# Reversed tables by wide copies, batches every 5.5 ticks, and the final weight on ScalarE, in a Hymba-style layer

## The chip, the cores and the metric

The kernel runs on one core of a Trainium2 chip (trn2). The core has TensorE for matrix products (PE in the profile, its weight loads PEld), VectorE (DVE), ScalarE (ACT), GpSimd (POOL) and SyncE (SP), which issues the DMAs; each has its own instruction stream and they meet at semaphores. The metric is the device time of one execution in microseconds (us). The kernel before ran three times: 1730.94, 1727.21 and 1730.14 us, median 1730.14.

## The reference

One decoder layer in float32, one batch of 1024 tokens, model width 1024, FFN width 2816. The code below is cut to what is computed.

```python
mod = silu(cond) @ w_mod + b_mod                       # 9 vectors: shift, scale, gate of 3 sub-layers
h = modulate(rms_norm(x, ffn1_norm), sh1, sc1)
x = x + 0.5 * g1 * ((silu(h @ w_gate) * (h @ w_up)) @ w_down)

h = modulate(rms_norm(x, mix_norm), sh2, sc2)
b_gate, c_gate, v, u = split(h @ w_in)                 # four parts of width 512
y_conv = b_gate * conv3_causal(c_gate * v)
y_ssm = s5_mixer(u)                                    # state_t = A state_{t-1} + B u_t, then GELU and a gate (GLU)
y_mix = concat(rms_norm(y_conv, out_norm_conv), rms_norm(y_ssm, out_norm_ssm))
x = x + g2 * (y_mix @ w_out)

h = modulate(rms_norm(x, ffn2_norm), sh3, sc3)
x = x + 0.5 * g3 * ((silu(h @ ffn2_w_gate) * (h @ ffn2_w_up)) @ ffn2_w_down)
return rms_norm(x, final_norm)
```

The S5 mixer has 32 groups of 16 channels with 64 complex states each. Its matrices depend only on weights (lambda, log_dt, B and C), so they can be made before `u` is known.

## The kernel before, in words

Activations lie transposed: eight tiles `xt` of x, in pairs, each of 128 features by 512 tokens for either half `h` of the tokens. The products run as three passes with operands split into a high and a low part (`mm3`: high by high, high by low, low by high), so a product of a 512-wide tile is 3 matmuls, and a sum over four tiles of features is 12.

The gate and up products of the first FFN go by a Strassen-Winograd scheme of seven products in place of eight (`seven`). A group of the FFN's width (fa0 to fa10 in the names, fb0 to fb10 for the second FFN) has seven products for the gate and seven for the up part, named by their blocks: fa5gB, fa5gD, fa5gA, fa5gE, fa5gC and so on. Each goes into a PSUM bank, and VectorE adds the banks together (`fa5gu<-fa5gt,fa5gB`); while a sum is still to be read, its bank is not free for the product that comes two or more later. The weights come by DMA as `raw`; GpSimd makes the sums of blocks that the scheme needs (the lines L165, L166, L174 and L176 of the profile); ScalarE casts each to a high part (`CAST w<-raw`), and VectorE subtracts this from `raw` for the low part (`TENSOR_TENSOR w<-raw,w`).

Nothing is reordered by a scheduler. The engine handles V, A, SP and T are wrapped by `InOrder`, which makes each instruction follow the one recorded before it on its engine, so an instruction stands behind all that the program gave to its engine earlier; every wrapped instruction bears the line of that helper in the profile, L108. What the order is made by is `Clock` (L60 to L100): one tick is one `mm3`. At each tick the clock runs what is due (`clock.after(ticks, fn)`), and at every `period` ticks it takes one step of the generators in `clock.side`. A group is 56 ticks, and each tick is 3 matmuls.

In the first FFN the side generator is `side1`: after the inputs' combinations it runs `ssm_base`, which makes the tables of the state-space model, and then `ssm_batch` for eight batches of four groups of channels each. `ssm_base` computes powers `pw` of the states' factors on VectorE and writes four tables `tab0` to `tab3` with ScalarE, two of them in the order of the powers and two reversed. `ssm_batch` builds its operands `cl` and `bl` (from the tables and the parameters `prm` and `bb`), asks TensorE for the products `kp` and for transposes `tp`, and rotates matrices (`rot`, `rott`); `dg` and `kc` put the diagonal in, and the results go to DRAM. The period is 4.5 ticks for all of this, and 2 from the last group's first half on.

In the second FFN's last down product (`fb10d`) the tail is made by `after2`: for each tile of x that is done, ScalarE squares it (`Sumsq.add`), and the squares are summed by GpSimd or VectorE and then by TensorE with a vector of ones (`st`). `roots` makes the reciprocal root in nine small VectorE instructions, `wide` spreads it over 128 columns (`rb`), and `spread` transposes it on TensorE into PSUM (`bc`). Then `put` multiplies each tile of x by the final weight (a column of `cols`) and by `bc`, and every second tile is followed by the DMA of both to the output. The first half of the tokens (n_0) is one piece of 512; the second is two pieces of 256, which the profile calls n_0 (128x256) and n_256.

Of the kernel before, what the change touches and what calls it, by code (L numbers as in the profile page):

```python
# [13 lines left out]
F32 = mybir.dt.float32  # L14
F32R = mybir.dt.float32r
I32 = mybir.dt.int32
AF = mybir.ActivationFunctionType
ALU = mybir.AluOpType
# [3 lines left out]
P = 128  # L22
D = 1024
S = 1024
HALF = 512
# [72 lines left out]
class InOrder:  # L98
# [4 lines left out]
    def __init__(self, tc, engine):  # L103
        self.tc, self.engine, self.last = tc, engine, None

    def __getattr__(self, name):
        def call(*args, **kw):
            r = getattr(self.engine, name)(*args, **kw)  # L108
            if self.last is not None and InOrder.strict:
                info = mybir.DependencyInfo(mybir.DependencyClass.NoSync, mybir.DependencyReason.DATA)  # L110
                self.tc.add_manual_dep(r.ins, self.last.ins.name, info, reason="order of issue")
            self.last = r
            return r

        return call
# [117 lines left out]
def hymba_layer(ctx: ExitStack, tc, x_d, wm1_d, wmod_d, gu1_d, gs1_d, ds1_d, wl1_d, win_d, wout_d, glu_d, gu2_d, gs2_d, wd2_d, ds2_d, wl2_d, cols_d, cond_d, lam_d, bc_d, out_d):  # L233
# [160 lines left out]
    def roots(st, q, width, nm):  # L394
# [13 lines left out]
        return y  # L408

    def wide(y, nm):  # L410

        q = y.shape[1]
        rb = t2k(nm + "rb")[:, : q * P].rearrange("p (a b) -> p a b", a=q)
        V.tensor_scalar(out=rb, in0=y.unsqueeze(2).to_broadcast([P, q, P]), scalar1=0.375, scalar2=None, op0=ALU.mult)
        return rb
# [528 lines left out]
    def ssm_base(sb, sb1):  # L944
# [114 lines left out]

        tabs = [sb.tile([P, 9, G], F32, tag=f"tab{i}", name=f"tab{i}") for i in range(4)]  # L1060
        for n, (t, (top, ts_, bot, bs_)) in enumerate(zip(tabs, ((0, 1, 1, -1), (1, -1, 0, -1), (0, 1, 1, 1), (1, -1, 0, 1)))):
            for part, i, sg in ((lo, top, ts_), (hi, bot, bs_)):
                if n < 2:
                    A.activation(t[part], pw[part, i], AF.Copy, scale=float(sg))
                else:

                    for q in range(8):
                        A.activation(t[part, q, :], pw[part, i, 7 - q, :], AF.Copy, scale=float(sg))
                yield
        zero = sb1.tile([CH, 112], F32, name="zero")  # L1070
# [135 lines left out]
    def side1():  # L1206
        yield from combos1()
        sb = side_open.enter_context(tc.tile_pool(name="sb", bufs=1, side="right"))
        with tc.tile_pool(name="sb1", bufs=1, side="right") as sb1:
            yield from ssm_base(sb, sb1)  # L1210
        bps.append(side_open.enter_context(tc.tile_pool(name="bp", bufs=1, side="right")))
        mod_home.pool = side_open.enter_context(tc.tile_pool(name="wmp", bufs=1, side="right"))
        for _ in range(2):
            mod_fetch(mod_home)
        for b in range(NB):
            yield from ssm_batch(b)
# [42 lines left out]
    movs["B"] = es1.enter_context(tc.tile_pool(name="movB1", bufs=12))  # L1259
    LAST_PERIOD = 2  # L1260
    sums_open, first_open = ExitStack(), ExitStack()
# [374 lines left out]
    down7("fbd1", lefts[1], 2, fetch_last)  # L1636
    n4 = {}
    WHOLE = [slice(0, HALF)]
    PIECES = (WHOLE, [slice(0, HALF // 2), slice(HALF // 2, HALF)])

    def after2(d, h, tok):
# [3 lines left out]
        ss = n4[h, tok.start]  # L1645
        ss.add(x[d][h][:, tok], apart=d == KT - 1, beside=d < 6)

        def put(k, bc):
            xs = x[k][h][:, tok]
            V.scalar_tensor_tensor(out=xs, in0=xs, scalar=cols[:, C_NF + k : C_NF + k + 1], in1=bc[:, :n], op0=ALU.mult, op1=ALU.mult)  # L1650
            if k % 2:
                SP.dma_start(out_d[h, :, k - 1 : k + 1, tok], xt[k // 2][h][:, :, tok])

        def use(bc):
            for k in range(KT):
                clock.after(2 * k, lambda k=k: put(k, bc))

# [96 lines left out]
```

## Time and profile before

| what | value |
| --- | --- |
| median of three runs | 1730.14 us (1727.21 to 1730.94) |
| the profiled execution | 1728.82 us |
| its span, first to last instruction | 1727.0 us |
| mean granted TensorE clock | 0.989 of full speed |
| busy: PE, PEld, DVE, ACT, POOL | 1661.6, 1368.2, 1263.0, 604.6, 373.8 us |
| DMA | 281.47 MB, mean 163 GB/s |

The profile has a page (busy times, slices, groups of instructions) and answers on the trace. In a row of the timeline stand the start, the time, the engine, the line, the operation, and output and inputs with their shapes; a count x12 says that so many equal instructions in a row are one row; in brackets stands the idle time of the engine before it and what ended it. Instructions on an engine overlap a little: the next one starts before the previous one's time is over. In the rows of waits stand the total, the count and the longest. In the rows of windows each engine's busy time is followed by its count; PEclk is the granted clock, 1.00 is full speed.

### The profile page before, as it was taken

Reading aid. Unit: us, or ns where it says so; the run is one execution under the profiler, and the core shown is the slowest. Engines: PE = TensorE matmul, PEld = TensorE weight load, DVE = VectorE, ACT = ScalarE, POOL = GpSimd, SP = SyncE. Lnnn points to the kernel's source line nnn. Section 1 sums busy time; section 2 is a strip of 40 time slices with the busy share of each in tenths; the row PEclk is TensorE's granted clock in tenths of the full one; section 3 lists DMA queues with packets and bytes.
Section 4 is the critical chain, followed back from the end, with each engine's and each line's share of the span. In section 5 each row is a group of like instructions: output and inputs, shape, how many; then the busy total and the mean of one; then the engine's idle time right before and its main releaser. Section 6 shows DMA issues by size and latency. Waiting matters only on the chain.

```text
span 1727.0 us, 20694 instructions
## 1 busy us (share of the span) xinstructions
PE 1661.6 (96%) x7484; PEld 1368.2 (79%) x7484; DVE 1263.0 (73%) x1994; ACT 604.6 (35%) x1032; POOL 373.8 (22%) x290
## 2 busy tenths in 40 slices
PE   4999999989999999999999899999999999999997
PEld 3787788878878878887877778888888888888886
DVE  7939789997589997644666877967776767676646
ACT  4225433333354332332113324533434443322221
POOL 0012232332322221100000021123223223332211
PEclk9999999999999999999999999999999999999998
DMA  8122364454564656225654452314444344659312
GB/s 326 77 98 96 131 217 156 153 186 136 213 210 151 228 183 253 67 69 151 208 164 135 150 186 90 141 49 171 177 190 170 147 156 161 260 227 375 112 49 98
DMA packets 101624, 281.47 MB, mean 163 GB/s; under 512 B 19345, under 2 KB 34961, under 8 KB 90386
## 3 DMA queue, kind: packets, MB, share of 16 engines
q1 hardware_dynamic: 101522, 280.15, 46.2%
q8 instruction: 59, 0.97, 0.2%
q14 instruction: 43, 0.35, 0.1%
HBM read 195.69 MB, written 76.02 MB: 157 GB/s over the span
## 4 chain that ended last, share of the span: by engine, by line
PE 48%; DVE 5%; DMA 3%; issue 1%; ACT 0%; SPq 0%; POOL 0%; DVEq 0%; ACTq 0%
PE wo L108 2%; PE fb10d L108 2%; PE u L108 2%; PE fbd_1B L108 2%; PE fbd_0B L108 2%; PE b L108 2%; PE v L108 1%; DMA swz<-si 1%; PE fb0u L108 1%; PE fbd_0A L108 1%; PE fb0g L108 1%; PE fbd_1C L108 1%; PE fbd_0C L108 1%; PE fbd_1A L108 1%; PE fb0d L108 1%; DMA wm<-in_wmod 1%
## 5 line engine op out<-in xcount | busy, mean ns | idle before, releaser
L108 ACT CAST w<-raw 128x512 fp32r<-128x512 f32 (+1 forms) x374 | 240.5, 677 | 474.8 <-issue 78.2
L108 DVE TENSOR_TENSOR w<-raw,w 128x512 fp32r<-128x512 f32 (+1 forms) x374 | 307.8, 843 | 123.0 <-ACT w L108 122.4
L174 POOL TENSOR_TENSOR raw<-sums,raw 128x512 f32<-128x512 f32 x54 | 81.3, 1505 | 415.4 <-DVE w L108 403.1
L165 POOL TENSOR_TENSOR sums<-raw 128x512 f32<-128x512 f32 x54 | 77.5, 1435 | 332.2 <-DMA raw<-in_gs 162.9
L176 POOL TENSOR_TENSOR raw<-raw 128x512 f32<-128x512 f32 x54 | 83.5, 1548 | 92.6 <-DVE w L108 92.6
L108 DVE CUSTOM_DVE_ANT_0 wm<-wm,cact 128x1024 f32<-128x1024 f32 x56 | 78.1, 1408 | 10.3 <-DMA wm<-in_wmod 10.2
L166 POOL TENSOR_TENSOR raw<-raw 128x512 f32<-128x512 f32 x54 | 84.5, 1564 | 4.2
L367 POOL TENSOR_TENSOR n3aq<-n3aq,n3aq 128x512 f32<-128x512 f32 x5 | 7.6, 1529 | 278.4 <-ACT n3aq L108 278.2
L108 PE MATMUL p<-h,w 128*128 128x512 f32 x192 | 49.2, 420 | 7.7 <-DVE h L108 5.4
L108 DVE TENSOR_TENSOR w<-sums,w 128x512 fp32r<-128x512 f32 x54 | 55.0, 1030 | 1.6 <-ACT w L108 1.0
L108 PEld LDWEIGHTS p<-h,w 128*128 128x128 f32 x192 | 38.9, 204 | 17.9 <-DVE h L108 6.4
L108 PE MATMUL wo<-oa,w 128*128 128x512 f32 x192 | 46.1, 393 | 1.2 <-DVE w L108 0.7
L108 PE MATMUL v<-h,w 128*128 128x512 f32 x192 | 46.8, 395 | 0.0
L108 PE MATMUL c<-h,w 128*128 128x512 f32 x192 | 46.6, 394 | 0.0
L108 PE MATMUL u<-h,w 128*128 128x512 f32 x192 | 45.9, 399 | 0.2 <-DVE h L108 0.2
L108 PE MATMUL b<-h,w 128*128 128x512 f32 x192 | 45.6, 393 | 0.0
L108 PE MATMUL wo<-ob,w 128*128 128x512 f32 x192 | 45.3, 391 | 0.0
L108 ACT CAST w<-sums 128x512 fp32r<-128x512 f32 x54 | 32.8, 621 | 34.5 <-PE fa9gE L108 2.2
L108 PEld LDWEIGHTS wo<-oa,w 128*128 128x128 f32 x192 | 35.7, 188 | 9.7 <-DVE w L108 1.1
L108 PEld LDWEIGHTS u<-h,w 128*128 128x128 f32 x192 | 36.3, 191 | 8.5 <-DVE h L108 0.6
L108 PEld LDWEIGHTS wo<-ob,w 128*128 128x128 f32 x192 | 35.8, 188 | 7.3
L108 PEld LDWEIGHTS b<-h,w 128*128 128x128 f32 x192 | 35.5, 188 | 7.2
(1579 smaller groups left out, 4004.4 us busy)
## 6 DMA issues: line engine op xcount, KB each, us to landing
raw<-in_gs SPq DMA_DIRECT2D x38, 1024.0 KB, 5.4
wm<-in_wmod SPq DMA_DIRECT2D x56, 512.0 KB, 4.9
raw<-in_ds SPq DMA_DIRECT2D x16, 1024.0 KB, 6.3
mw<-in_wm SPq DMA_DIRECT2D x8, 1024.0 KB, 12.4
x<-in_x SPq DMA_DIRECT2D x16, 512.0 KB, 9.0
raw<-in_win SPq DMA_DIRECT2D x8, 1024.0 KB, 5.4
raw<-in_gu SPq DMA_DIRECT2D x6, 1024.0 KB, 10.2
raw<-in_wl SPq DMA_DIRECT2D x5, 1024.0 KB, 6.5
```

What stands on the lines that cost most here:

```text
L108: r = getattr(self.engine, name)(*args, **kw)
L165: self.G.tensor_tensor(out=f, in0=r[2], in1=r[1], op=ALU.subtract)
L166: self.G.tensor_tensor(out=r[1], in0=r[1], in1=r[0], op=ALU.subtract)
L174: self.G.tensor_tensor(out=r, in0=s["t3"], in1=r, op=ALU.add)
L176: self.G.tensor_tensor(out=r, in0=self.chunk(j, 3), in1=r, op=ALU.subtract)
L367: nc.gpsimd.tensor_tensor(out=a, in0=a, in1=sq[:, :n], op=ALU.add)
```

## The change

There are three edits. First, the two reversed tables: before, 32 small ScalarE instructions of 64x32 each read one power at a time; now eight copies of 128x2x32 fill a tile `pd` with the powers in reversed order, and four instructions of 64x256 write the tables from it. The generator yields twice among the copies and after each table, 6 times instead of 8. Second, from the end of `ssm_base` the side period is 5.5 ticks instead of 4.5. Third, in the tail ScalarE multiplies each finished tile by the final weight right behind its square, so `put` is one multiplication by `bc` for a pair of tiles (128x1024, or 128x2x256) and the pair's DMA; the squares of the seventh tile are added by GpSimd; and the writing of the second half's first piece is split, with its last two pairs made to follow the last piece's `rb`.

```diff
     class InOrder
+    def follow(self, r, before):
+        info = mybir.DependencyInfo(mybir.DependencyClass.NoSync, mybir.DependencyReason.DATA)
+        self.tc.add_manual_dep(r.ins, before.ins.name, info, reason="order of issue")
...
     def wide(y, nm):
-        V.tensor_scalar(out=rb, in0=y.unsqueeze(2).to_broadcast([P, q, P]), scalar1=0.375, scalar2=None, op0=ALU.mult)
+        r = V.tensor_scalar(out=rb, in0=y.unsqueeze(2).to_broadcast([P, q, P]), scalar1=0.375, scalar2=None, op0=ALU.mult)
+        widened.append(r)
         return rb
...
         tabs = [sb.tile([P, 9, G], F32, tag=f"tab{i}", name=f"tab{i}") for i in range(4)]
+        down_ = sb1.tile([P, 2, 8, G], F32, tag="pd", name="pd")
+        for q in range(8):
+            A.copy(down_[:, :, q, :], pw[:, :, 7 - q, :])
+            if q % 4 == 3:
+                yield
         for n, (t, (top, ts_, bot, bs_)) in enumerate(zip(tabs, ((0, 1, 1, -1), (1, -1, 0, -1), (0, 1, 1, 1), (1, -1, 0, 1)))):
             for part, i, sg in ((lo, top, ts_), (hi, bot, bs_)):
                 if n < 2:
                     A.activation(t[part], pw[part, i], AF.Copy, scale=float(sg))
                 else:
-
-                    for q in range(8):
-                        A.activation(t[part, q, :], pw[part, i, 7 - q, :], AF.Copy, scale=float(sg))
-                yield
+                    A.activation(t[part, 0:8, :], down_[part, i], AF.Copy, scale=float(sg))
+            yield
...
             yield from ssm_base(sb, sb1)
+        clock.period = BATCH_PERIOD
...
-    LAST_PERIOD = 2
+    LAST_PERIOD, BATCH_PERIOD = 2, 5.5
...
-        ss.add(x[d][h][:, tok], apart=d == KT - 1, beside=d < 6)
-
-        def put(k, bc):
-            xs = x[k][h][:, tok]
-            V.scalar_tensor_tensor(out=xs, in0=xs, scalar=cols[:, C_NF + k : C_NF + k + 1], in1=bc[:, :n], op0=ALU.mult, op1=ALU.mult)
-            if k % 2:
-                SP.dma_start(out_d[h, :, k - 1 : k + 1, tok], xt[k // 2][h][:, :, tok])
+        xs = x[d][h][:, tok]
+        ss.add(xs, apart=d == KT - 1, beside=d < 7)
+        A.activation(xs, xs, AF.Copy, scale=cols[:, C_NF + d : C_NF + d + 1])
+
+        def put(j, bc):
+            pair = xt[j][h][:, :, tok]
+            r = V.tensor_tensor(out=pair, in0=pair, in1=bc[:, :n].unsqueeze(1).to_broadcast([P, 2, n]), op=ALU.mult)
+            if h and tok.start == 0 and j > 1:
+                V.follow(r, widened[-1])
+            if h and tok.start and j == 0:
+                V.follow(r, put_last[-1])
+            put_last.append(r)
+            SP.dma_start(out_d[h, :, 2 * j : 2 * j + 2, tok], pair)

         def use(bc):
-            for k in range(KT):
-                clock.after(2 * k, lambda k=k: put(k, bc))
+            back = 7 if h and tok.start == 0 and n < HALF else 2
+            for j in range(KT // 2):
+                clock.after((1 if back > 2 else 4) * j + back, lambda j=j: put(j, bc))
```

The order of the program shows three places. On ScalarE, where the tables are made during group fa3, before (the names are those of the tables `tab`, the powers `pw` and the split weights `w`; the number behind a name is a buffer's):

```order
L108 COPY fa3gt_1321<-fa3gA 128x512
L108 ACTIVATE tab_1523<-pw 64x288
L108 ACTIVATE tab_1524<-pw 64x288
L108 ACTIVATE tab_1523<-pw 64x288
L108 CAST w_1344<-raw_1039 128x512
L108 CAST w_1344<-raw_1165 128x512
L108 ACTIVATE tab_1524<-pw 64x288
L108 ACTIVATE tab_1525<-pw 64x32 x16
L108 ACTIVATE tab_1526<-pw 64x32 x16
L108 CAST w_1400<-raw_1165 128x512 x2
```

and now:

```order
L112 COPY fa3gt_1321<-fa3gA 128x512
L112 ACTIVATE tab_1523<-pw 64x288
L112 ACTIVATE tab_1524<-pw 64x288
L112 COPY pd<-pw 128x2x32 x2
L112 CAST w_1344<-raw_1039 128x512
L112 CAST w_1344<-raw_1165 128x512
L112 COPY pd<-pw 128x2x32 x6
L112 ACTIVATE tab_1523<-pw 64x288
L112 ACTIVATE tab_1524<-pw 64x288
L112 ACTIVATE tab_1525<-pd 64x256 x2
L112 ACTIVATE tab_1526<-pd 64x256 x2
L112 CAST w_1400<-raw_1165 128x512 x2
```

Between the two pairs of casts stood 33 instructions, and there are 12 now.

On VectorE, at the first batch's second block in group fa5 (`dg` to `clt` are the batch's; the two `fa5gu` additions and `fa5gt` read the banks of that group's products), before:

```order
L108 TENSOR_SCALAR gate<-gate 128x8
L108 TENSOR_TENSOR fa5gu_2094<-fa5gu_2079,fa5gD 128x512
L108 TENSOR_TENSOR w_2098<-raw_1838,w_2098 128x512
L108 TENSOR_TENSOR fa5gt_2030<-fa5gu_2094,fa5gC 128x512
L108 TENSOR_TENSOR w_2098<-raw_1838,w_2098 128x512
L108 TENSOR_TENSOR dg_2162<-ident,lam 16x64
L108 TENSOR_TENSOR bb_2194<-prm_2191,qq 128x128
L108 TENSOR_TENSOR kc_2160<-kc_2160,dg_2162 16x4x16
L108 TENSOR_TENSOR bb_2195<-prm_2191,qq 128x128
L108 TENSOR_TENSOR bb_2193<-bb_2194,bb_2195 128x64 x2
L108 TENSOR_TENSOR cl_2200<-tab_1523,prm_2191 128x576
L108 TENSOR_TENSOR clt_2201<-tab_1524,prm_2191 128x576
```

and now:

```order
L112 TENSOR_SCALAR gate<-gate 128x8
L112 TENSOR_TENSOR dg_2130<-ident,lam 16x64
L112 TENSOR_TENSOR bb_2172<-prm_2169,qq 128x128
L112 TENSOR_TENSOR kc_2128<-kc_2128,dg_2130 16x4x16
L112 TENSOR_TENSOR bb_2173<-prm_2169,qq 128x128
L112 TENSOR_TENSOR bb_2171<-bb_2172,bb_2173 128x64 x2
L112 TENSOR_TENSOR cl_2178<-tab_1523,prm_2169 128x576
L112 TENSOR_TENSOR clt_2179<-tab_1524,prm_2169 128x576
L112 TENSOR_TENSOR fa5gu_2088<-fa5gu_2060,fa5gD 128x512
L112 TENSOR_TENSOR w_2092<-raw_1835,w_2092 128x512
L112 TENSOR_TENSOR fa5gt_2015<-fa5gu_2088,fa5gC 128x512
L112 TENSOR_TENSOR w_2092<-raw_1835,w_2092 128x512
```

The batch's block has moved from behind `fa5gt` to ahead of it. Over the whole first FFN the batches' products `kp` stand 22 to 36 ticks apart before, three of them in group fa7, and 27 to 44 apart now, two at most in a group.

On VectorE at the program's end (the last two pieces; `n_1_0` and `n_1_256` are the program's names for what the profile calls n_0 and n_256), before:

```order
L108 SCALAR_TENSOR_TENSOR x_1_3800<-x_1_3800,cols,n_1_0bc 128x256
L108 SCALAR_TENSOR_TENSOR n_1_256ny<-n_1_256na,n_1_256ni 128x2
L108 SCALAR_TENSOR_TENSOR x_1_3800<-x_1_3800,cols,n_1_0bc 128x256
L108 TENSOR_TENSOR n_1_256na<-n_1_256ny 128x2
L108 TENSOR_TENSOR n_1_256na<-n_1_256na,n_1_256nv 128x2
L108 SCALAR_TENSOR_TENSOR n_1_256na<-n_1_256na 128x2
L108 SCALAR_TENSOR_TENSOR n_1_256ny<-n_1_256na,n_1_256ny 128x2
L108 TENSOR_SCALAR n_1_256rb<-n_1_256ny 128x256
L108 SCALAR_TENSOR_TENSOR x_1_3797<-x_1_3797,cols,n_1_256bc 128x256 x2
```

and now:

```order
L112 SCALAR_TENSOR_TENSOR n_1_256ny<-n_1_256na,n_1_256ny 128x2
L112 TENSOR_SCALAR n_1_256rb<-n_1_256ny 128x256
L112 TENSOR_TENSOR x_1_3780<-x_1_3780,n_1_0bc 128x2x256
L112 TENSOR_TENSOR x_1_3781<-x_1_3781,n_1_0bc 128x2x256
L112 TENSOR_TENSOR x_1_3778<-x_1_3778,n_1_256bc 128x2x256
```

The multiplications of the second half's first piece, which stood between the steps of the last piece's root, now stand half ahead of them and half behind `rb`.

More of the change, by code (lines that the diff above doesn't have):

```diff
@@ L109, in call @@
             if self.last is not None and InOrder.strict:
-                info = mybir.DependencyInfo(mybir.DependencyClass.NoSync, mybir.DependencyReason.DATA)
-                self.tc.add_manual_dep(r.ins, self.last.ins.name, info, reason="order of issue")
+                self.follow(r, self.last)
             self.last = r
@@ L408, in roots @@
         return y
+    widened = []
     def wide(y, nm):
@@ L1636, in hymba_layer @@
     down7("fbd1", lefts[1], 2, fetch_last)
-    n4 = {}
+    n4, put_last = {}, []
     WHOLE = [slice(0, HALF)]
```

## The prediction

> **What bounds the kernel now.** I read the page's busy times first, then the waits of TensorE, then a timeline at each long wait. TensorE:
>
> ```profile
> span 1727.0 us, 20694 instructions
> PE 1661.6 (96%) x7484; PEld 1368.2 (79%) x7484; DVE 1263.0 (73%) x1994; ACT 604.6 (35%) x1032; POOL 373.8 (22%) x290
> ...
> PE kp L108 <- DVE bl L108: 4.5, 2, 4.2
> ...
> PE fa3gC L108 <- DVE fa3gt L108: 3.4, 1, 3.4
> ...
> PE fad_0A L108 <- DVE w L108: 2.7, 2, 2.0
> ```
>
> TensorE is busy for 1661.6 of 1727.0 us, so whatever an edit saves must come out of the 65.4 us in which it idles, out of time in which it runs at a lower clock, or out of what follows its last matmul. The change adds and removes no multiplication on TensorE. Two of its places stand in these rows (wait in total, count, longest): `kp`, a batch's products, and `fa3gC`, both waiting for VectorE. The third is the tail. I take the three in turn.
>
> **Tables (first edit).** In the timeline around 181 us ScalarE makes the four tables while TensorE wants a bank:
>
> ```profile
> 181.32 4.60 ACT L108 ACTIVATE tab<-pw 64x288 f32<-64x288 f32 x33
> ...
> 181.71 2.88 PE L108 MATMUL fa3gE<-h,w 128*128 128x512 f32 x12
> ...
> 185.94 1.14 ACT L108 CAST w<-raw 128x512 fp32r<-128x512 f32 x2
> 186.59 0.69 DVE L108 TENSOR_TENSOR w<-raw,w 128x512 fp32r<-128x512 f32 x1 [2.85 <-ACT w L108]
> ...
> 187.20 0.68 DVE L108 TENSOR_TENSOR fa3gt<-fa3gu,fa3gC 128x512 f32<-128x512 f32 x1
> ...
> 188.03 4.41 PE L108 MATMUL fa3gC<-h1S,w 128*128 128x512 f32 x12 [3.44 <-DVE fa3gt L108]
> ...
> 190.58 1.76 DVE L108 TENSOR_TENSOR w<-raw,w 128x512 fp32r<-128x512 f32 x1
> ...
> 192.23 3.11 PE L108 MATMUL fa3uA<-h,w 128*128 128x512 f32 x12
> ...
> 195.18 1.07 PE L108 MATMUL fa3uC<-h1S,w 128*128 128x512 f32 x4
> ```
>
> The weight casts wait on ScalarE behind 33 small instructions (4.60 us). VectorE, in its order, stands at the `w` that needs the cast (2.85 us idle) with `fa3gt` behind it, and TensorE's second `fa3gC` needs the bank that `fa3gt` reads. Then the clock falls. In the windows (TensorE's busy time first, granted clock as PEclk near the end of a row):
>
> ```profile
> 190.00:192.00 2.00, 2.00 (x6) 1.54 (x6) 2.00 (x2) 0.59 (x2) 1.79 (x2) 0.50 0.15 31
> ...
> 388.00:390.00 2.00, 1.73 (x8) 1.01 (x8) 1.97 (x4) 0.00 (x0) 0.00 (x0) 0.50 0.72 295
> ...
> 392.00:394.00 2.00, 2.00 (x7) 1.52 (x6) 1.46 (x3) 1.69 (x4) 0.00 (x0) 0.50 0.71 162
> ...
> 620.00:622.00 2.00, 1.47 (x6) 1.24 (x7) 2.00 (x3) 0.00 (x0) 1.91 (x2) 1.00 0.00 0
> ```
>
> After 3.44 us of idling it is 0.50 at 190 to 192; after the 2.0 us of `fad_0A`, which ended at 620.5, it stayed 1.00. Twelve matmuls at full clock take 2.72 us (fa5gE to fa5gC below, 264.77 to 267.50). From 188.03 to 195.18 two sets took 7.15 us in place of 5.44: 1.71 lost to the clock, with the idling 5.15 us in all.
>
> What the new order costs, by the two groups that ran in that stretch (busy time, mean of one):
>
> ```profile
> L108 ACT ACTIVATE tab<-pw 64x32 f32<-64x32 f32 x32 | 4.2, 213 | 0.0
> ...
> L108 ACT ACTIVATE tab<-pw 64x288 f32<-64x288 f32 x4 | 1.7, 438 | 5.3 <-DVE pw L108 5.2
> ```
>
> Back to back, 32 elements take 4.2/32 = 0.131 us and 288 take 1.7/4 = 0.425. On the line between them 64 elements (one `pd` copy) take 0.17 and 256 take 0.39. Between the two pairs of casts now stand six copies, two 288s and four 256s: 6×0.17 + 2×0.425 + 4×0.39 = 3.4 us instead of 4.6; ahead of the first pair two copies replace one 288 (0.34 for 0.425). The casts start 1.2 + 0.1 = 1.3 us earlier, VectorE was waiting for nothing else, and the idling falls from 3.44 to about 2.1. That is next to the 2.0 that kept the clock, so I take 2.1 as the whole loss: **gain 3.0**. Bounds: 1.3 if the clock falls all the same, 5.15 if nothing of the wait is left. The two yields that fall away move the batches' start by a tick or two only; the second edit sets the period from there.
>
> The Trainium skill, "TensorE: Matmul & The Clock Gate", Part 1, says that the clock is halved after an idle window of about 3.4 us and that the window runs freely, which the 3.44 here fits, and the 3.53 in the tail; by a free-running window a 2.1 us gap is mostly, not surely, safe. No sum uses it.
>
> **Batches (second edit).** A batch of the SSM's matrices is spread over steps between the matmuls, with about 10 us of VectorE. Windows of one group of 168 matmuls each (the third figure after the comma is VectorE's, with its count):
>
> ```profile
> 211.50:249.60 38.10, 38.10 (x170) 31.55 (x169) 32.51 (x50) 12.10 (x21) 12.18 (x7) 1.00 0.60 208
> 249.60:290.80 41.20, 41.20 (x193) 33.52 (x192) 39.96 (x61) 14.16 (x25) 13.05 (x9) 1.00 0.50 173
> 290.80:332.00 41.20, 41.20 (x188) 33.81 (x187) 36.68 (x60) 13.55 (x24) 12.64 (x8) 1.00 0.47 154
> 332.00:373.70 41.70, 41.38 (x199) 33.29 (x198) 39.85 (x64) 15.29 (x27) 12.47 (x8) 1.00 0.52 158
> 373.70:424.60 50.90, 46.71 (x205) 37.57 (x204) 40.53 (x69) 16.56 (x29) 13.43 (x9) 0.93 0.44 142
> 424.60:459.99 35.39, 35.39 (x157) 29.28 (x156) 20.29 (x30) 10.32 (x18) 11.32 (x8) 1.00 0.68 260
> ```
>
> The last has no batch: 20.29 in 35.39, or 21.8 in the 38.1 of a group. The five with batches hold 189.5, less 5×21.8 leaves 80.5 for eight batches, 10 each (some of that is the gates' rows). Before, group fa7 holds three batches' products: 21.8 + 30 = 52 of VectorE in a stretch of some 42, so VectorE falls behind, and the next batch's product pays:
>
> ```profile
> 386.97 1.16 DVE L108 TENSOR_TENSOR bl<-bl,blt 128x512 f32<-128x512 f32 x1
> ...
> 388.27 1.86 PE L108 MATMUL kp<-cl,bl 128*16 128x128 f32 x8 [4.19 <-DVE bl L108]
> ```
>
> Idle 4.19 us, then half clock from 388.3 to 394 (rows above): half of 5.7 is 2.9. With the other wait of `kp` (4.5 − 4.2 = 0.3) the loss is 7.4; the sets that were not quite at half speed take about 0.3 off it, so 7.1. At 5.5 ticks a step no group holds more than two products: 21.8 + 20 = 42 in about 41. That is level, not behind. I take all 7.1 as gained; bounds 0 (VectorE falls behind elsewhere) and 7.4. The batches end some 15 us later, in the stretch of the last window above where VectorE is 57% busy, and the next thing that needs their results comes only after this stage; I cost that at nothing, and were that cover gone it would show as a wait of the mixer.
>
> What the new steps meet: the order shows the first batch's block (`dg`, `bb`, `kc`, `bb`, `bb` twice, `cl`, `clt`) now ahead of the additions that free the bank of the second `fa5gC`; before it stood behind them.
>
> ```profile
> 262.36 1.29 POOL L174 TENSOR_TENSOR raw<-sums,raw 128x512 f32<-128x512 f32 x1 [10.28 <-DVE w L108]
> ...
> 264.77 2.88 PE L108 MATMUL fa5gE<-h,w 128*128 128x512 f32 x12
> 264.98 0.68 DVE L108 TENSOR_TENSOR fa5gt<-fa5gu,fa5gC 128x512 f32<-128x512 f32 x1
> ...
> 267.50 2.88 PE L108 MATMUL fa5gC<-h1S,w 128*128 128x512 f32 x12
> ...
> 268.13 2.52 DVE L108 TENSOR_TENSOR bb<-bb,bb 128x64 f32<-128x64 f32 x2
> ...
> 338.47 0.21 DVE L108 TENSOR_TENSOR dg<-ident,lam 16x64 f32<-16x64 f32 x1
> ...
> 341.12 1.29 DVE L108 TENSOR_TENSOR w<-raw,w 128x512 fp32r<-128x512 f32 x2
> ```
>
> The same block undisturbed took 341.12 − 338.47 = 2.65 us. `fa5gt` ended at 265.66; with the block ahead it ends at 268.3, and `fa5gC`, ready at 267.50, waits 0.9 with the release. But GpSimd works around this time (its addition of 262.36 ends at 263.65, and others follow), and two-input work of VectorE is at times longer: the `bb` pair here took 2.52 us, as much as the whole block elsewhere, and the `w` of 190.58 took 1.76 where that of 186.59 took 0.69, 1.1 more. With one such stretch between the block and `fa5gt` the wait is 0.9 + 1.1 = 2.0 to 2.05, which I take (2.05), since the block itself would mostly run in the gap behind 263.65. Bounds: 0.9, and 5 if the whole block is stretched as the `bb` pair was (2.2 more) with the clock falling. Net of this edit: 7.1 − 2.05 = **5.05**.
>
> The Trainium skill, "GPSIMD Engine Reference", says that GpSimd shares its SBUF interfaces with VectorE, and that two-SBUF-input instructions of VectorE contend; the rows agree (1.76 against 0.69), though they do not say which of its instructions did it, and no number above needs it.
>
> **The tail (third edit).** VectorE's end, after TensorE's last product:
>
> ```profile
> 1715.92 0.15 DVE L108 TENSOR_SCALAR n_256nv<-n_256st 128x2 f32<-128x2 f32 x1
> ...
> 1718.41 0.16 DVE L108 TENSOR_TENSOR n_256na<-n_256na,n_256nv 128x2 f32<-128x2 f32 x1
> ...
> 1719.00 0.29 DVE L108 TENSOR_SCALAR n_256rb<-n_256ny 128x256 f32<-128x256 f32 x1
> ...
> 1719.35 1.22 PE L108 MATMUL n_256bc<-ident,n_256rb 128*128 128x128 f32 x4 [3.53 <-DVE n_256rb L108]
> 1720.61 3.22 DVE L108 SCALAR_TENSOR_TENSOR x<-x,cols,n_256bc 128x256 f32<-128x256 f32 x8 [1.32 <-PE n_256bc L108]
> ```
>
> Between 1715.92 and 1719.00 nine small instructions of the root alternate with multiplications of the previous piece; the change sends two of the four paired ones behind `n_256rb`. Uninterleaved, nine follow each other at 0.2 us, as the last three before `n_256rb` do (1718.41 to 1719.00): 1716.2 + 1.8 = 1718.0 (1716.2 since the two paired writes ahead end some 0.3 later). `n_256bc` arrives 1719.65, and four multiplications of 512 elements, each about 0.6 apart (`fa5gt`, which also reads PSUM, started 264.98 and took 0.68, of which some 0.08 overlaps the next), end at 1722.1 rather than 1720.61 + 3.22 = 1723.83. The two pairs moved behind lie in the wait for `n_256bc`. The span ends 3.17 us after the last multiplication, for the transfers; the same transfers now start closer together, so not all of the 1.7 reaches the end: **gain 1.5**, bounds 0 (transfers decide) and 2.2. ScalarE's 24 added multiplications (a pair of its 512-wide casts took 1.14, so some 0.6 each) lie beside 2.72 us of matmuls per tile; the addition moved to GpSimd also ends before its piece's sums.
>
> **The sum.** 3.0 + 5.05 + 1.5 = 9.55 us off the span, 1727.0 to 1717.4. The profiled execution took 1728.82, 1.8 around its span and 1.3 under the median of 1730.14; so about 1719.3 for such an execution and 1730.14 − 9.55 = **1720.5** for a median.
>
> **The rivals.** Prices are against 1730.14 or the forecast.
>
> (1) *The clock still falls at the tables* (the gate's rule above says when): gain 1.3 there, not 3.0; 1722.3. For it: 2.1 is above 2.0, the only gap seen to be harmless. Chance 0.15.
>
> (2) *The wait at fa5gC is 5 us, or one like `kp`'s returns once more* as VectorE stays level but not ahead: 3 to 7 us more; 1723.5 to 1727.5. For it: two batches need 42 in 41. Against: a group without batches follows. Chance 0.2.
>
> (3) *Slower.* Blocks of a batch stand ahead of bank-freeing additions in every group, not in fa5 alone. Each such place that idles TensorE over 3.4 us costs 5.15, as at the tables. Without the wait at fa5gC the forecast would be 1718.45; three such places make 1733.9, which is slower by the bound below, four 1739.1. For it: the steps fall at other places of a group each time. Against: `fa5gt` ended 1.8 us before `fa5gC` was ready, so a block of 2.65 alone costs only 0.9. Chance 0.06.
>
> (4) *The tail is bound by transfers and the batches' gain is as forecast*: 1722.0. Chance 0.1, inside the range.
>
> **How the numbers follow.** The forecast itself (1717 to 1722) has 0.49. The range runs from all terms at their good end (5.15 + 7.4 − 0.9 + 2.2 = 13.9, 1716.3; some 1.3 more for the spread of the runs, 1727.21 to 1730.94, so 1715) to most of rival 2: 1726. What a measurement of this kernel can tell from no change is 0.2%, 3.5 us: faster means below 1726.7. Faster 0.82 (forecast 0.49, rivals 1 and 4 0.25, the lower part of rival 2, 0.08), same 0.12 (its upper part), slower 0.06.
>
> **What would show it.** Right: `fa3gC`'s wait near 2.1 and clock 1.00 at 188 to 194; no wait of `kp` over 1 us; a new wait of `fa5gC` near 2; `n_256rb` near one us earlier relative to `n_256nv`. Wrong: a row of 0.50 after the tables, a `kp` or bank wait over 3.4 us in fa5 to fa9, or a span that ends as long after `n_256bc` as before.

## The result and the profile after

The changed kernel took 1721.68 us, the median of five runs (1719.28 to 1722.76), against 1730.14 of the kernel before (1727.21 to 1730.94, five runs). The ratio is 0.9951, with a 95% interval of 0.9937 to 0.9966: faster by 8.5 us. The forecast was 1720.5, within 1715 to 1726. One later execution of the changed kernel ran at a clock of 0.656 throughout and took 2395.23 us; it stands outside every comparison. The profiled execution took 1719.28, its span 1717.5.

The page's first lines of the profile after:

```profile
span 1717.5 us, 20689 instructions
...
PE 1657.8 (97%) x7484; PEld 1365.9 (80%) x7484; DVE 1262.0 (73%) x1979; ACT 616.0 (36%) x1036; POOL 375.3 (22%) x293
```

VectorE has as much to do as before (1262.0 us for 1263.0); what fell is TensorE's time, idle (59.7 for 65.4) and busy at a low clock. TensorE's waits in the profile after (total, count, longest):

```profile
PE n_0bc L112 <- DVE n_0rb L112: 2.4, 1, 2.4
...
PE fa3gC L112 <- DVE fa3gt L112: 2.3, 1, 2.3
PE n_256bc L112 <- DVE n_256rb L112: 2.2, 1, 2.2
...
PE fa10uC L112 <- DVE fa10ut L112: 2.0, 1, 2.0
...
PE fa5gC L112 <- DVE fa5gt L112: 1.5, 1, 1.5
```

`kp` is gone from the list, `fa3gC` is 2.3 for 3.4, and `fa5gC` is new: the three things that the prediction named. `fa10uC` with 2.0 was not foreseen. For the comparison by place I cut each profiled execution at five instructions that stand in all of them, by their starts in the timeline: the first fa3gA, the first fa5gA, the first fa9uA, the first `wo` (the output projection of the mixer) and TensorE's last product fb10d. In us:

| stretch | before | after | first edit alone | the same, steps put back | block behind fa5gt | period 5.0 |
| --- | --- | --- | --- | --- | --- | --- |
| fa3gA to fa5gA (tables) | 81.46 | 78.70 | 78.68 | 78.71 | 80.22 | 78.73 |
| fa5gA to fa9uA (batches) | 191.38 | 185.77 | 193.06 | 190.73 | 184.00 | 196.82 |
| fa9uA to wo | 511.57 | 513.17 | 511.98 | 514.24 | 510.66 | 520.65 |
| wo to the last product | 758.64 | 756.57 | 756.59 | 757.06 | 758.39 | 759.42 |
| last product to the end | 15.84 | 15.30 | 16.49 | 15.75 | 14.5 | 14.46 |

Between before and after the batches give 5.6, the tables 2.8 and the tail 0.5; and of the two stretches between, which no edit touches, one loses 1.6 and the other gains 2.1. The rows behind the first three, in the timeline of the profile after:

```profile
182.96 1.69 ACT L112 ACTIVATE tab<-pd 64x256 f32<-64x256 f32 x4
184.67 1.14 ACT L112 CAST w<-raw 128x512 fp32r<-128x512 f32 x2
185.32 0.69 DVE L112 TENSOR_TENSOR w<-raw,w 128x512 fp32r<-128x512 f32 x1 [1.73 <-ACT w L112]
...
186.76 2.97 PE L112 MATMUL fa3gC<-h1S,w 128*128 128x512 f32 x12 [2.28 <-DVE fa3gt L112]
...
260.90 0.20 DVE L112 TENSOR_TENSOR dg<-ident,lam 16x64 f32<-16x64 f32 x1
...
262.87 0.75 DVE L112 TENSOR_TENSOR clt<-tab,prm 128x576 f32<-128x576 f32 x1
263.54 0.68 DVE L112 TENSOR_TENSOR fa5gu<-fa5gu,fa5gD 128x512 f32<-128x512 f32 x1
...
264.14 1.35 DVE L112 TENSOR_TENSOR w<-raw,w 128x512 fp32r<-128x512 f32 x1
...
265.42 0.68 DVE L112 TENSOR_TENSOR fa5gt<-fa5gu,fa5gC 128x512 f32<-128x512 f32 x1
...
266.24 3.00 PE L112 MATMUL fa5gC<-h1S,w 128*128 128x512 f32 x12 [1.49 <-DVE fa5gt L112]
...
344.41 1.05 PE L112 MATMUL kp<-cl,bl 128*16 128x128 f32 x8
```

The casts start at 184.67 for 185.94. The `fa3gC` behind them takes 2.97 us for its twelve matmuls where it took 4.41 before: the clock stayed up. The batch's block (260.90 to 263.54, 2.64 us) stands ahead of fa5gt, one `w` is stretched to 1.35, and TensorE idles 1.49. The products `kp` come with no idle time before them.

The two stretches that no edit touches differ by where the clock fell. In the profile after it fell behind the 1.96 us of `fa10uC`, in the third stretch (timeline):

```profile
488.98 4.47 PE L112 MATMUL fa10uC<-h1S,w 128*128 128x512 f32 x12 [1.96 <-DVE fa10ut L112]
```

Before, this wait was 0.88 and the twelve matmuls took 3.00. The order of work is the same there; what came late is a transfer. ScalarE's cast of a weight, which had waited for its DMA, started 0.52 us behind the start of `fa10uE`, where it had started 0.57 ahead of it before (484.66 and 484.14 after, 492.06 and 492.63 before), and `fa10ut` stands behind that weight's low part on VectorE. So here TensorE came 8.5 us earlier and the data only 7.4. With the falls in the mixer the third stretch has two after (490 to 494 and, at `gl`, 934 to 938) and one before (738 to 742). In the fourth stretch it was the other way: a window of the profile before, behind the first products `wo`, has a clock of 0.66,

```profile
970.00:975.00 5.00, 5.00 (x21) 4.03 (x20) 4.89 (x9) 1.23 (x2) 0.00 (x0) 0.66 0.67 207
```

and at the same place after (958 to 973) none is below 1.00. In both profiles TensorE idles 2.30 us there ahead of the matmuls `nBabc`; the clock fell behind it in one and not in the other.

### The profile page after: what moved, and what is told of

Its sections match the earlier page's. It is cut to its first block, busy times and chain, and to the rows that moved or that the text cites. A ratio compares the mean times of both kernels' runs of the same rounds, so it can differ in the third digit from the quotient of the medians.

```text
span 1717.5 us, 20689 instructions
## 1 busy us (share of the span) xinstructions
PE 1657.8 (97%) x7484; PEld 1365.9 (80%) x7484; DVE 1262.0 (73%) x1979; ACT 616.0 (36%) x1036; POOL 375.3 (22%) x293
## 4 chain that ended last, share of the span: by engine, by line
PE 50%; DVE 4%; DMA 3%; issue 0%; ACT 0%; SPq 0%; DVEq 0%; ACTq 0%
PE wo L112 4%; PE fb10d L112 2%; PE u L112 2%; PE fbd_1B L112 2%; PE fbd_0B L112 2%; PE b L112 2%; PE v L112 1%; DMA swz<-si 1%; PE fb0u L112 1%; PE fbd_0C L112 1%; PE fbd_1C L112 1%; PE fbd_1A L112 1%; PE fb0d L112 1%; PE fb0g L112 1%; PE fbd_0A L112 1%; PE gl L112 1%
```

## Experiments

Eleven altered kernels ran, and the changed kernel once more. Each ratio is to runs of the kernel before, made beside it on the same chip; 0.2% is about what the whole time can tell, so effects of 1 or 2 us are read from the stretches above.

**The first edit alone.** Diff: the change's hunk on `down_` and `tabs`, nothing else.

> The kernel before with the first edit alone (pd copies, wide tables, 6 yields for 8). Theory: TensorE's wait for fa3gt falls from 3.44 to about 2.3 us, the clock stays 1.00 behind it, and some 2.9 us come off the span; the wait of kp in group fa8 (4.19) is not touched, about 4, unless the two yields fewer move the batches' steps. Rival (the clock falls all the same): 1.2 us. Rival (parts overlap: the tables' gain is lost in a later wait for VectorE): 0. A median near 1727.2.

Measured: ratio 1.0011 (0.9992 to 1.0029), no gain, though the profiled execution shows the tables' stretch 2.8 us shorter. The next stretch took 1.7 of it back (193.06 for 191.38); in the timeline of this kernel:

```profile
186.25 2.96 PE L108 MATMUL fa3gC<-h1S,w 128*128 128x512 f32 x12 [2.27 <-DVE fa3gt L108]
...
266.66 4.57 PE L108 MATMUL fa5gC<-h1S,w 128*128 128x512 f32 x12 [2.42 <-DVE fa5gt L108]
...
384.37 1.03 PE L108 MATMUL kp<-cl,bl 128*16 128x128 f32 x8 [2.56 <-DVE bl L108]
...
417.35 3.00 PE L108 MATMUL fa8uC<-h1S,w 128*128 128x512 f32 x12 [1.64 <-DVE fa8ut L108]
```

The edit has two yields fewer, every batch stands two steps earlier, its block comes ahead of fa5gt, and fa5gC waits 2.42 us and then runs at half clock (4.57 for twelve). The rival "lost in a later wait for VectorE" is what this run showed for the larger part of the 2.8; where the rest went in the median is not shown.

**The first edit with the steps put back.** Is it the moved steps, or would the gain be lost in any case?

```diff
             yield
+        yield
+        yield
         zero = sb1.tile([CH, 112], F32, name="zero")
```

> The first edit alone with two empty yields put back behind the tables, so that the batches stand exactly where they stood in the kernel before. Theory: by itself the first edit gained nothing (ratio 1.0011) because two yields fewer move every batch: its block came ahead of fa5gt, and fa5gC waited 2.42 us with the clock at half. With the steps put back that wait goes and the 2.9 us of the tables are seen: median 1726.5, ratio 0.9983, kp's wait of about 4 as before. Rival (the time won at the tables is lost in any case further on): ratio 1.000.

Measured: ratio 0.9992 (0.9975 to 1.0009). The interval holds both expectations. The trace is clearer: fa5gC no longer waits, `kp` waits 4.2 as before, and the first two stretches together are 269.44 us, 3.4 less than before (272.84), where with the moved steps they were 271.74, 1.1 less. So the moved steps cost 2.3 us of these stretches. That the whole time gains 2.9 with the steps put back is not shown: its interval is too wide.

**The period alone.** Diff: `clock.period = BATCH_PERIOD` with 5.5, nothing else.

> The kernel before with the second edit alone (side period 5.5 from the end of the tables on). Theory: the 4.19 us wait of kp and the half clock behind it are gone, about 7 us; and since the block of the first batch stands behind fa5gt in this program's order, the new wait at fa5gC does not come, so 7 and not 5. Median near 1723. Rival (VectorE's arrears move, they do not go): a wait over 3 us at another kp or bank, gain under 3.

Measured: median 1722.77, ratio 0.9964 (0.9951 to 0.9978), so about 6.2 us. TensorE has no wait for VectorE from 196 to 480 us in this trace, no `kp` and no `fa5gC`. The profiled execution itself was the longest of its ten (1728.95), by falls of the clock elsewhere: at 890, 939 and 969 us, behind 2.42 us of `yy`, 1.73 of `gl` and 2.30 of `nBabc`; and `fa3gC` at the tables took 5.46 for 4.41, which makes that stretch 82.66. The stretch of the batches is 182.42 here, and the two together are 7.8 less than before. The expected 7 is within the interval (3.8 to 8.5).

**The tail alone.** Diff: the change's hunks on `follow`, `widened` and `after2`.

> The kernel before with the third edit alone. Theory: as in the changed kernel's tail, 15.8 us from the start of TensorE's last six products to the end become 15.3, so 0.5 us, since the wide multiplications of the first half's tokens hold the root of n_0 up by 0.4 and TensorE's clock falls before n_0bc and n_256st. Rival (the tail by itself gains the 1.5 that was forecast and only another place in the changed kernel takes it back): 14.3. Median 1729 to 1730.

Measured: ratio 0.9987 (0.9974 to 0.9999), 2.2 us; from the last product to the end 14.44 us, 1.4 less than before. That is the rival's number. The difference to the changed kernel is the clock. TensorE's last rows in this kernel's timeline:

```profile
1711.56 0.88 PE L112 MATMUL fb10d<-fb_1a,w 128*128 128x256 f32 x6
1714.79 0.71 PE L112 MATMUL n_0bc<-ident,n_0rb 128*128 128x128 f32 x4 [2.35 <-DVE n_0rb L112]
1715.34 0.95 PE L112 MATMUL n_256st<-one,n_256q 128*128 128x1 f32 x8
1718.92 1.22 PE L112 MATMUL n_256bc<-ident,n_256rb 128*128 128x128 f32 x4 [2.63 <-DVE n_256rb L112]
```

and in the changed kernel's:

```profile
1702.20 0.88 PE L112 MATMUL fb10d<-fb_1a,w 128*128 128x256 f32 x6
1705.43 1.23 PE L112 MATMUL n_0bc<-ident,n_0rb 128*128 128x128 f32 x4 [2.35 <-DVE n_0rb L112]
1706.45 1.71 PE L112 MATMUL n_256st<-one,n_256q 128*128 128x1 f32 x8
1710.38 1.22 PE L112 MATMUL n_256bc<-ident,n_256rb 128*128 128x128 f32 x4 [2.23 <-DVE n_256rb L112]
```

The idle time before n_0bc is 2.35 us in both. In one execution n_0bc took 0.71 and n_256st 0.95, in the other 1.23 and 1.71. In the executions with the edited tail and a clock that stayed up through n_0bc the end took 14.44 to 14.5 us, in those where it fell 15.30 and 15.32; with the tail of before it took 15.75 to 15.84 and 16.49 by the same two cases. Like with like, the edit gains about 1.2 to 1.3.

**The block behind fa5gt.** The changed kernel; the batch's first block must follow fa5gt on VectorE.

```diff
+            if self.behind is not None:
+                self.follow(r, self.behind)
...
                     add(t1, u3, "C")
+                    marks[nm] = V.last
...
+        V.behind = marks["fa5g"] if b == 0 else V.behind
         dg = bt(f"dg{b}")
...
             V.tensor_tensor(out=t, in0=la[1], in1=sc[1], op=ALU.mult)
+            V.behind = None
```

> The changed kernel, with the first batch's block (dg to clt) made to follow fa5gt on VectorE. Theory: the wait of 1.49 us at fa5gC goes and nothing takes its place, since the block's products are due later: 1.5 us off the changed kernel. Rival (the block only moves the delay to the additions of fa5gE behind it, or to the next kp): 0.

Measured: median 1719.52, ratio 0.9951 (0.9935 to 0.9968), which the whole time cannot tell from the changed kernel. The stretch of the batches is 184.00 for 185.77, 1.8 less, and the wait at fa5gC is not in the trace; nor is a wait of 2 us at fa10uC (0.5). So the wait does cost its 1.5 to 1.8 us and nothing takes its place there. This kernel's trace has a second finding, at the tables:

```profile
186.93 4.45 PE L112 MATMUL fa3gC<-h1S,w 128*128 128x512 f32 x12 [2.31 <-DVE fa3gt L112]
```

and a window just behind (the clock is the third number from the end):

```profile
188.00:190.00 2.00, 2.00 (x6) 1.59 (x5) 1.53 (x2) 1.49 (x3) 1.92 (x2) 0.50 0.18 39
```

The code there is the changed kernel's, and the idle time is 2.31 for 2.28. Yet here the clock fell.

**A longer wait at the tables.** The changed kernel with four more copies on ScalarE:

```diff
+        for q in range(4):
+            A.copy(down_[:, :, q, :], pw[:, :, 7 - q, :])
```

> The changed kernel with four of the eight pd copies made twice (ScalarE 0.65 us longer between the two pairs of casts). Theory of a fixed threshold between 2.28 and 3.44: the wait at fa3gC becomes 2.9; if the threshold is near 3.4 the clock stays 1.00 and the cost is 0.65 us. Rival (the clock is judged in windows that run freely, so a shorter wait can also lower it): at 2.9 it falls in some executions, in the profiled one perhaps, with 1.5 us more and a wider spread of the runs.

Measured: ratio 0.9957 (0.9943 to 0.9971), the whole time as the changed kernel's. In the profiled execution `fa3gC` idled 2.87 us and then took 4.21, with a clock of 0.50 from 190 to 192: fallen. One execution cannot tell a threshold below 2.9 from chance, but the runs together exclude one length of idle time that decides at every place. The idle time ahead of twelve matmuls of fa3gC, fa5gC and fa10uC and what they took, from thirteen profiles:

| idle, us | took about 3.0 (clock up) | took 4.2 to 5.5 (clock fell) |
| --- | --- | --- |
| 1.48 to 1.81 | 1.48, 1.49, 1.52, 1.63, 1.78 | 1.81 |
| 1.96 to 2.13 | none | 1.96, 2.13 |
| 2.27 to 2.33 (fa3gC) | 2.27, 2.27, 2.28, 2.28, 2.29, 2.30 | 2.31, 2.33 |
| 2.42 to 2.87 | 2.45 | 2.42, 2.87 |
| 3.44 to 3.48 | none | 3.44, 3.45, 3.48 |

At fa3gC by itself the two that fell, 2.31 and 2.33, are also the two longest of the eight, so these eight alone would allow a threshold there; at fa10uC 1.96 fell and 2.45 did not.

**TensorE kept busy in the tail.** The changed kernel, with small matmuls into a bank that nobody reads:

```diff
+            if h and tok.start:
+                warm(10)
+                clock.after(7, lambda: warm(7))
...
+    def warm(n):
+        t = ps("warm")
+        for i in range(n):
+            before = T.last
+            r = T.matmul(t[:, i % 4 * P : (i % 4 + 1) * P], lhsT=ident[:], rhs=ident[:], start=True, stop=True)
+            T.follow(r, before)
```

> The changed kernel, with 10 small matmuls into a bank that nobody reads between TensorE's last product and n_0bc, and 7 between n_256st and n_256bc. Theory: the tail's gain was 0.5 and not 1.5 because TensorE's clock fell in the idling of 2.35 us: n_0bc 1.23 us instead of 0.71, n_256st 1.71 instead of 1.28. Kept busy, it stays at 1.00: n_0bc near 0.7, n_256st below 1.0, n_256bc near 0.7, 1.2 to 1.7 us off the time from the last product to the end (15.3). Rival (these times are set by the waits and the transfers, not by the clock): 15.3 again.

Measured: ratio 0.9954 (0.9938 to 0.9971); from the last product to the end 14.47 us (1705.73 to 1720.2), 0.8 less than the changed kernel's 15.30. n_0bc took 0.71, n_256st 0.95 and n_256bc 0.71, as expected, but the gain is 0.8 and not 1.2 to 1.7: the root, VectorE's multiplications and the transfers behind n_256bc are as long as before. It is also what the changed tail takes by itself when the clock does not fall at n_0bc (14.44 to 14.5): the small matmuls take away the fall and nothing beyond it.

**The last piece's sums first.** The changed kernel, with n_256st ahead of n_0bc on TensorE and all four multiplications of the piece before behind n_256rb:

```diff
-            if h and tok.start == 0 and j > 1:
+            if h and tok.start == 0:
                 V.follow(r, widened[-1])
...
-            ss.rstd(D, use, 6, 11)
+            ss.rstd(D, use, 0 if h and tok.start else 6, 11)
...
+            before = T.last
+            r = T.matmul(bc[:, i * P : (i + 1) * P], lhsT=rb[:, i, :], rhs=ident[:], start=True, stop=True)
+            if nm == "n4_1_0":
+                T.follow(r, before)
```

> The changed kernel, with the last piece's sums n_256st made ahead of n_0bc on TensorE, and all four multiplications of the piece before put behind n_256rb. Theory: the root of the last piece is what the end hangs on; its sums start at once when the squares are there (0.6 earlier and not behind 1.2 us of n_0bc), n_256bc comes 1.5 us earlier, but VectorE then has eight multiplications (5 us) behind it, so 0.7 us off the time from the last product to the end (15.3). Rival (VectorE's work is what the end hangs on): 0 or a loss.

Measured: 14.1 us from the last product to the end, 1.2 less than 15.30 (0.7 was expected); ratio 0.9962 (0.9944 to 0.998), the whole time again unable to tell. The clock was up at n_0bc in this execution (0.69 us), so like with like, against 14.44 to 14.5, the new order gives 0.3 to 0.4. Here VectorE sets the end:

```profile
1716.43 0.29 DVE L112 TENSOR_SCALAR n_256rb<-n_256ny 128x256 f32<-128x256 f32 x1
1716.64 2.47 DVE L112 TENSOR_TENSOR x<-x,n_0bc 128x512 f32<-128x512 f32 x4
1719.04 2.47 DVE L112 TENSOR_TENSOR x<-x,n_256bc 128x512 f32<-128x512 f32 x4
```

The eight multiplications follow each other without a gap from 1716.64 to 1721.5.

**A period of 5.0.** Diff: `BATCH_PERIOD` 5.0 in the changed kernel.

> The changed kernel with a side period of 5.0 instead of 5.5. Theory (VectorE's arrears over a group): products of three batches fall into group fa8 again, but after those no further product waits, and no other group has three; VectorE is some 10 us short only at the end, so kp waits less than 2 us and the loss against 5.5 is 0 to 3 us. The block of the first batch stands ahead of the bank's additions again, so a wait at fa5gC of 1 to 3 us stays. Rival (only a period of 5.5 or more keeps VectorE level): kp's wait of 4 and the half clock come back, 7 us.

Measured: ratio 0.9995 (0.998 to 1.001): all that the change won is lost. In the trace the waits for VectorE are back:

```profile
268.15 4.56 PE L112 MATMUL fa5gC<-h1S,w 128*128 128x512 f32 x12 [2.13 <-DVE fa5gt L112]
377.63 1.31 PE L112 MATMUL kp<-cl,bl 128*16 128x128 f32 x8 [1.98 <-DVE bl L112]
401.40 1.19 PE L112 MATMUL kp<-cl,bl 128*16 128x128 f32 x8 [2.16 <-DVE bl L112]
421.49 1.03 PE L112 MATMUL kp<-cl,bl 128*16 128x128 f32 x8 [1.23 <-DVE bl L112]
```

The three products of group fa8 wait one after the other, 5.4 us in all, the clock falls behind two of them and behind fa5gC, and the stretch of the batches is 196.82 us. I had expected 0 to 3 us of loss, since no product follows the third; it is 11 in this execution (the longest of its ten) and 6 to 7 in the median (1729.01 for 1722.44 of the changed kernel beside it). The rival was nearer, though the waits are 2 and not 4.

**The changed kernel again, and two that join the repairs.** The changed kernel ran once more beside two that have all of these together: the block behind fa5gt, the last piece's sums first, and 8 small matmuls ahead of the sums and 8 ahead of n_256bc; in the second, also 12 ahead of the second fa3gC and 10 ahead of the first `gl`:

```diff
+    def nm_fill(name, side, n):
+        return (name, side, n) == ("fa3", "g", 6)
...
+                if nm_fill(name, side, n):
+                    warm(12)
                 for k in range(4):
...
         ready(actG, h, 4)
+        if not h:
+            warm(10)
```

> The changed kernel once more, unaltered, for more runs on the same chip as the next three. Theory: ratio 0.995 to the kernel before; in the profiled execution the wait at fa3gC is 2.3 us again, and the clock behind it is 1.00 or 0.50 by chance, as in the seven executions seen with about 2.3 us of idling there, where it fell in two. Rival (the same program idles and falls in the same way each time): 1.00, as in the first profile.

> The changed kernel with the three repairs together: the first batch's block behind fa5gt, the last piece's sums ahead of n_0bc with all writing of the piece before behind n_256rb, and 8 small matmuls into an unread bank ahead of the sums and 8 ahead of n_256bc. Theory: the waits are apart in time, so they add: 1.5 and about 1.5 more (the 1.2 measured for the sums' order, and half of n_256bc's 1.2), near 1718.5, ratio 0.9935. Rival (the spread of the clock hides it): no difference from the changed kernel.

> As the last, and TensorE kept busy in two more gaps: 12 small matmuls ahead of the second fa3gC (idle 2.3 us) and 10 ahead of the first gl (idle 1.7). Theory (an idle time of 1.7 to 2.4 us lowers the clock in some executions and not in others): fewer falls, some 1 us less on average (1.7 us at fa3gC in about two of seven, 1.7 at gl in most), and a narrower spread; in the profile the windows behind fa3gC and gl show 1.00. Rival (the falls come from elsewhere, or the small matmuls delay their successors): the same as the last, or slower by 0.5.

Measured: the changed kernel 1722.44 us, ratio 0.996 (0.9948 to 0.9973); the execution with a trace is the one of 2395.23 us, so the question of chance at fa3gC rests on the other runs. The first joined kernel: 1719.62, ratio 0.9945 (0.9927 to 0.9963). The second: 1718.05, ratio 0.9932 (0.9917 to 0.9948), 12 us below the kernel before. Its interval and the changed kernel's touch at 0.9948 and do not overlap otherwise; its six runs lie within 1716.12 to 1720.24, where ten of the changed kernel beside it lie within 1718.9 to 1726.55. The two joined kernels' intervals overlap, so what the last two fillings add is not shown by the whole time. The gap at the tables in its timeline (each small matmul stands in it as two):

```profile
184.61 2.84 PE L112 MATMUL warm<-ident 128*128 128x128 f32 x24
187.20 3.02 PE L112 MATMUL fa3gC<-h1S,w 128*128 128x512 f32 x12
```

and the clock is 1.00 in the windows from 186 to 192 and, at `gl`, from 930 to 942, where the first joined kernel has 0.60 and 0.55 (932 to 940). In the tail the small matmuls gave nothing beside the sums' order: 14.16 and 14.12 us from the last product to the end, against 14.1 without them. There n_256bc is ready early, and VectorE's eight multiplications decide.

## Why the prediction was right

**The tables.** Forecast 3.0 us, measured 2.8 in the stretch. The sizes held: 1.69 us for four 64x256 instructions (0.42 each, 0.39 forecast), eight copies 1.4 us, the wait 2.28 for 2.1. But the step "2.1 is next to the 2.0 that kept the clock, so I take 2.1 as the whole loss" was weaker than its chance of 0.15 for rival 1 said. Of eight profiled executions with 2.27 to 2.33 us there, the clock fell in two. The 2.0 was also not the only gap of its size in the profile before: behind the 2.30 us ahead of `nBabc` the clock there was 0.62 from 970.66 to 971.66 and then 0.50, and behind the 1.94 ahead of n_0bc it was 0.50 from 1715.0 on, so before the 3.53 in the tail began. By these rows the chance should have been set higher. The gain is about 2.8 in three of four executions and about 1.3 in the fourth (80.22 in the stretch for 78.70, with the same code there).

**"The two yields that fall away move the batches' start by a tick or two only"** was the step that failed. I costed it at nothing. By itself it brought the block ahead of fa5gt and cost the first edit 2.3 of its 2.8 us (271.74 for 269.44 with the steps put back). In the whole change it is the reason for the wait at fa5gC, which I had from the order of the program and priced at 2.05 (1.49 measured, since the stretched `w` took 0.67 longer and not 1.1): with the period alone the block stands behind fa5gt and the wait is not there. So the wait at fa5gC belongs to the first edit, not to the second as my sum had it; the sum of the two is the same.

**The batches.** Forecast 5.05 net, measured 5.6; of the 7.1 gross, 7.4 are had when the block is put behind fa5gt (191.38 to 184.00). The argument that VectorE must not have three batches in a group is borne out by the period of 5.0, and more sharply than I thought: short arrears already make waits of 1.2 to 2.2 us, and behind two of those three the clock fell.

**The tail.** Forecast 1.5, measured 0.5 in the first profile. The term was not mis-sized in its own parts: from n_256nv to n_256rb the time fell from 3.08 to 1.84 us, and the four multiplications took 2.48 for 3.22. What I left out is ahead of n_256nv: the 128x1024 multiplications of the first half's tokens stand between the steps of the root of n_0, and n_0bc came 3.23 us after the last product's start for 2.83. The idle time grew from 1.94 to 2.35, and in that execution the clock fell before n_0bc. Where it did not fall, the end took 14.44 for the 15.84 of before, 1.4 less. Rival 4, transfers that bound the tail, cost little: the span ended 3.38 us after the last multiplication for 3.17.

**The other rivals.** Rival 2's wait of 5 us at fa5gC did not come: 1.49 to 1.81 in the four profiles with the changed kernel's code there, with a fallen clock in one of them. `kp` waits in none of these. Rival 3, blocks ahead of the bank's additions in several groups, was not seen, neither at 5.5 nor at 5.0, where fa5gC alone waited so. What took the whole gain at 5.0 was rival 2's mechanism, products `kp` that wait for VectorE, and it lies half a tick away.

**The sum** came out at 9.5 us of span for 9.55 forecast, and 8.5 between the medians. That the span came so close is luck, for the terms did not: 0.2 too much for the tables, 0.55 too little for the batches, 1.0 too much for the tail, and 0.5 from two untouched stretches, which lost 1.6 (fa10uC, with the clock) and won 2.1. The Trainium skill, "TensorE: Matmul & The Clock Gate", Part 1, says that the clock is halved after an idle window of about 3.4 us and that the window runs freely. The table of idle times agrees with the second, with a fall at 1.81 and none at 2.45; it does not bear out the first as a bound, since gaps far below 3.4 us lowered the clock.

**A correction.** The description of the kernel before says that nothing is reordered by a scheduler. That is so only in the opening stage, where `InOrder.strict` is set. Elsewhere a scheduler at build time orders what is independent; the block of the batch came ahead of fa5gt by it, although the program gives it to VectorE later (the run with the block behind fa5gt could name fa5gt as already given), which is why `follow` is needed to hold it back.

## What to carry to other kernels

A side job that is issued at every so many ticks has two numbers to watch: how much of the helping engine's time it takes in one period of the main loop, and where in the period its pieces fall. Any edit that adds or removes a step moves all later pieces, and can cost more than the edit itself gains; an empty step keeps them in place. Compare stretches between fixed instructions before adding up terms, since a sum can be right by terms that cancel.

## What was not expected of the hardware

The same idle time of TensorE lowers the clock in one execution and not in the next, and the place counts for more than the length. The thirteen profiles have most of their waits at the same places; the table counts in how many of those that have the wait the clock was below 1.00 within 1.5 us behind it.

| first matmuls behind the wait | idle, us | profiles | clock fell in |
| --- | --- | --- | --- |
| `gl`, the first that waits | 1.71 to 1.75 | 12 | 10 |
| `nAbbc` | 1.74 to 1.75 | 13 | 0 |
| `fad_0A` | 1.95 to 2.01 | 12 | 2 |
| second fa3gC, new tables | 2.27 to 2.33 | 8 | 2 |
| `nBabc` | 2.29 to 2.30 | 13 | 6 |
| n_0bc, new tail | 2.35 to 2.36 | 5 | 3 |

Three of these in the timeline of the profile after; only behind the first did the clock fall, and there 32 matmuls took 9.18 us for 7.56 before:

```profile
933.79 9.18 PE L112 MATMUL gl<-yg,w 128*128 128x512 f32 x32 [1.74 <-DVE yg L112]
944.72 1.16 PE L112 MATMUL nAbbc<-ident,nAbrb 128*128 128x128 f32 x8 [1.74 <-DVE nAbrb L112]
...
962.78 1.13 PE L112 MATMUL nBabc<-ident,nBarb 128*128 128x128 f32 x8 [2.30 <-DVE nBarb L112]
```

At 3.44 to 3.48 us ahead of fa3gC all three fell. Why `gl` falls so often and `nAbbc`, with the same idle time, never did is not shown. A fall costs about 1.4 us at twelve matmuls (4.4 for 3.0). Part of the runs' spread may come from it, and that is not shown either, nor that filling the gaps narrows the spread: six runs of the last kernel lie within 4.1 us, and so do ten of the tail alone.
